# An encoder block's opening: the first norm's gain row loaded into four partitions and spread by VectorE, TensorE given full warming products

## The chip, the core and the metric

The kernel runs on one core of a Trainium2 chip. The core has five engines with instruction queues of their own: TensorE (PE, matrix products; PEld is its weight load), VectorE (DVE), ScalarE (ACT), GpSimd (POOL) and SyncE (SP), which here only issues transfers. SBUF is the memory on chip that the engines work in (128 partitions), PSUM the memory of eight banks that TensorE writes its products to. Sixteen DMA engines move data between the chip's main memory and SBUF; SP, ACT and POOL can issue transfers. Engines wait for one another by semaphores, and each works through its own queue in order.

The metric is device time of one execution in microseconds, the median of several. A profile is one execution, seen by the hardware profiler.

## The reference

A sequence of 512 rows of width 1024 in float32 goes through a feed-forward layer, a mixer (a gated convolution beside a two-way chunked mLSTM) and a second feed-forward layer, each between two RMS norms:

```
def rmsnorm(x, g):
    x32 = x.astype(jnp.float32)
    y = x32 * lax.rsqrt(jnp.mean(x32 * x32, axis=-1, keepdims=True) + EPS)
    return (y * g.astype(jnp.float32)).astype(x.dtype)
...
        h = swiglu(rmsnorm(x, norm_ffn1_pre[l]), w_ffn1_in[l], w_ffn1_out[l])
        x = x + FFN_RESIDUAL_SCALE * rmsnorm(h, norm_ffn1_post[l])
        h = mixer(rmsnorm(x, norm_mix_pre[l]), w_mix_in[l], conv_w[l], ...)
        x = x + rmsnorm(h, norm_mix_post[l])
        h = swiglu(rmsnorm(x, norm_ffn2_pre[l]), w_ffn2_in[l], w_ffn2_out[l])
        x = x + FFN_RESIDUAL_SCALE * rmsnorm(h, norm_ffn2_post[l])
```

The opening, which the change touches, is the very first `rmsnorm(x, norm_ffn1_pre)` and the first columns of `w_ffn1_in`.

## The kernel before

The 512 rows of x stand in four blocks of 128 rows, block 0 to block 3, each a tile of 128 partitions by 1024. A product in float32 is made of three products of the split halves: `split` (L351 on) rounds a tensor to a high part on ScalarE (L352, `whi` for a weight, `big` for activations) and subtracts it for a low part (L355, on VectorE; for the first four weights on GpSimd, `wlo`). TensorE multiplies high by high, high by low and low by high.

The opening runs like this. `pre_norm` normalizes a block: ScalarE squares and sums its two halves (L382), VectorE makes the mean of it (L368, L371), GpSimd takes it to the power -0.5 (L375), and VectorE multiplies x by this scale and by the gain row, half by half (L450). The gain row `norm_ffn1_pre` is one row of 1024 numbers that every partition needs. SyncE loads it into one partition of the tile `g_row` (L321), first in its queue, ahead of x. TensorE spreads it: a product of a column of ones (`vrows`, one partition) with the row, one for each half, puts it into every partition of two PSUM banks, `g_pre` (L348). L450 reads the gain from there for all four blocks.

Around these two products stand 20 warming products of zeros (L345, operand `warm`, a bfloat16 view of `rawg`): 12 ahead of them and 8 behind. Then `flip_q` transposes block 0 and block 1 on TensorE (L407, four transposes to a half), and between the two blocks stand four further transposes into an unused bank (L755). The halves in PSUM are split into the activations' high and low parts (`big`), and a plain copy of them is kept (L413, for blocks 2 and 3 L416). Blocks 2 and 3 are normalized and flipped during the first four weights' products (L524), which take first the columns of blocks 0 and 1 for all four weights, then those of blocks 2 and 3. After that follow the products of a seven-product scheme (L498).

What sets the order: instructions marked `pin` keep the program's order on their engine, others are placed by a scheduler that works with the compiler's own times. SyncE issues g_row, x of blocks 0 and 1 (two halves each), two weights, x of block 2, a weight, x of block 3 and a weight; later weights wait for a free buffer of the pool `raw`. GpSimd's queue has, behind the constants, the powers of blocks 0 and 1, the splits of the first two weights, the power of block 2, the third split, the power of block 3 and the fourth split. The pool `gbp` has two buffers for gains; `g_row` is the first of them, in both kernels.

Of the kernel before, what the change touches and what calls it, by code (L numbers as in the profile page):

```python
# [16 lines left out]
P = 128  # L17
# [9 lines left out]
EPS = 1e-6  # L27
NEG = -1e30
SPLIT = ((8, 5), (8, 5))
WARM = 20  # L30
WARM2 = 4
ON_POOL = (0, 1, 2, 3)
PLAIN = 2
BW = 528
# [4 lines left out]
def encoder_kernel(ctx: ExitStack, tc: tile.TileContext, a: dict, out: bass.AP):  # L39
    nc = tc.nc  # L40
# [15 lines left out]
    def nm(s):  # L56
        uid[0] += 1
        return f"{s}_{uid[0]}"
# [4 lines left out]
    def ps():  # L63
        return psum.tile([P, 512], F32, tag="ps", name=nm("ps"))
# [13 lines left out]
    def blk(i, n=P):  # L78
        return slice(i * n, (i + 1) * n)
# [7 lines left out]
    def pin(ins):  # L87

        if pinned["PE" if ins.ins.engine == nc.tensor.engine else "rest"]:
            tc.keep_in_program_order(ins)  # L90
# [181 lines left out]
    def w_split(n):  # L272
        for _ in range(n):
            if not loaded:
                w_load(1)
            if not loaded:
                return
            raws, kk = loaded.pop(0)
            if isinstance(kk, str):
                ready.append((w_out_a if kk == "a" else w_out_b)(*raws))  # L280
                continue
            if len(raws) == 2:
                ready.append(w_pair(*raws))
                continue
            raw = raws[0]
            hi = wpool.tile([P, 1024], F32R, tag="w", name=nm("whi"))
            lo = wpool.tile([P, 1024], F32R, tag="w", name=nm("wlo"))
            eng = nc.gpsimd if done[0] in ON_POOL else nc.vector
            done[0] += 1
            split(hi, lo, raw, eng)  # L290
            if kk > 1:
                hi, lo = (v.rearrange("p (k f) -> p k f", k=kk) for v in (hi, lo))
            ready.append((hi, lo))
# [12 lines left out]
    def x_load(tb, parts=1):  # L306
        for i in range(parts):
            h = blk(i, D // parts)
            nc.sync.dma_start(x_t[tb][:, h], a["x"][0, blk(tb), h])
# [8 lines left out]
        return g  # L318

    g_row = gbp.tile([P, D], F32, tag="gb", name="g_row")  # L320
    nc.sync.dma_start(g_row[0:1, :], a["norm_ffn1_pre"])  # L321
    x_load(0, 2)
    x_load(1, 2)
    w_load(2)
# [6 lines left out]
    ident = const.tile([P, P], F32, name="ident")  # L331
# [4 lines left out]
    warm = rawg.rearrange("p k f -> p (k f)").bitcast(BF16)  # L336
    nc.gpsimd.memset(warm, 0.0)
    vrows = const.tile([20, P], F32, name="vrows")
    ones = vrows[0:1, :]
    nc.gpsimd.memset(ones, 1.0)  # L340
    pw = ps()
    first = [ps() for _ in range(4)]
    g_pre = [ps() for _ in range(2)]
    for n in range(WARM):
        pin(nc.tensor.matmul(pw[:, 0:256], warm[:, 0:P], warm, start=True, stop=True))  # L345
        if n == 11:
            for i in range(2):
                pin(nc.tensor.matmul(g_pre[i], ones, g_row[0:1, blk(i, 512)], start=True, stop=True))  # L348


    def split(hi, lo, src, eng=nc.vector):  # L351
# [49 lines left out]
    def flip_q(tb, xs, xq, halves=(0, 1), bank=None):  # L401

        full = []
        for b in halves:
            pt = bank or ps()
            for k in range(4):
                pin(nc.tensor.transpose(out=pt[:, blk(k)], in_=xs[:, blk(4 * b + k)], identity=ident))  # L407
            hi, lo = xq_hl(xq, (b, tb // 2))
            split(hi[:, :, blk(tb % 2)], lo[:, :, blk(tb % 2)], ch(pt))
            if b not in xq["f"]:  # L410
                xq["f"][b] = bigt()
            if bank:
                return lambda: pin(nc.vector.tensor_copy(xq["f"][b][:, :, blk(tb)], ch(pt)))  # L413
            full.append((b, pt))
        for b, pt in full:
            pin(nc.scalar.copy(xq["f"][b][:, :, blk(tb)], ch(pt)))  # L416
# [27 lines left out]
    def pre_norm(tb, g, parts=2):  # L444
        xs = t4()
        r = rstd([sumsq(x_t[tb][:, blk(i, D // parts)]) for i in range(parts)], D, 1.0)
        for i in range(2):
            h = blk(i, 512)
            gh = g[i] if isinstance(g, list) else g[:, h]
            pin(nc.vector.scalar_tensor_tensor(  # L450
                out=xs[:, h], in0=x_t[tb][:, h], scalar=r, in1=gh, op0=ALU.mult, op1=ALU.mult))
        return xs
# [295 lines left out]
    xs = [pre_norm(tb, g_pre) for tb in range(2)]  # L748
    full = []
    for tb in range(2):  # L750
        for b in range(2):
            full.append(flip_q(tb, xs[tb], xT1, (b,), first[2 * tb + b]))
        if tb == 0:
            for i in range(WARM2):
                pin(nc.tensor.transpose(out=pw[:, 0:P], in_=xs[0][:, blk(i % 4)], identity=ident))  # L755
        w_split(1)
    for fn in full:
        fn()
# [7 lines left out]
    def rows8(rows, base):  # L766
        v = ident[0:rows, base:base + 64].rearrange("p (d x) -> p d x", d=2)
        return v[:, :, 0:4]
# [3 lines left out]
        out=selc.rearrange("p (d h) -> p d h", d=2), in0=rows8(P, 0), in1=rows8(P, 64), op=ALU.add,  # L772
# [5 lines left out]
        out=pm, in_=selc[0:36].rearrange("p (d h) -> p h d", d=2), axis=AX.X, op=ALU.add,  # L778
# [3 lines left out]
        out=par, in_=selc[0:36].rearrange("p (d h) -> p d h", d=2), axis=AX.X, op=ALU.add,  # L782
# [67 lines left out]
    for tb in range(NT):  # L850
        pv_ = [ps(), ps()]
        n = 0
        for k in range(KD):
# [3 lines left out]
            for xx, ww in ((0, hi), (0, lo), (1, hi)):  # L857
                for i, at in enumerate((slice(0, 256), slice(256, BW))):
                    nc.tensor.matmul(  # L859
                        pv_[i][:, 0:at.stop - at.start], xv(xx, k, tb), ww[:, k % 2, at],  # L860
                        start=n == 0, stop=n == 3 * KD - 1)
# [281 lines left out]
    for c in range(NT):  # L1143
        for pr in range(2):
            nc.tensor.transpose(
                out=pkn[c // 2][:, blk(2 * (c % 2) + pr)], in_=kk_[:, pr, blk(c)], identity=ident,
# [5 lines left out]
    for c in range(NT):  # L1152
# [3 lines left out]
        start=True, stop=True,  # L1156
# [169 lines left out]
    xs = {}  # L1326
    for tb in range(NT):
        acc = [ps(), ps()]
        for half in range(2):
            for n, k in enumerate(MIXK):  # L1330
# [3 lines left out]
                for yi, wi in ((0, 0), (0, 1), (1, 0)):  # L1334
                    nc.tensor.matmul(  # L1335
                        acc[half], yy[yi][:, k % 4, blk(tb)], wmo[k][wi][:, blk(half, 512)],
                        start=(n == 0 and yi == 0 and wi == 0), stop=(n == 7 and yi == 1),
# [40 lines left out]
```

## Time and profile before

| what | value |
|---|---|
| median of 3 runs | 894.24 us (893.87 to 894.26) |
| the profiled execution | 893.36 us |
| its span, first to last instruction | 891.6 us |
| TensorE busy | 883.4 us, 99% |
| VectorE busy | 716.3 us, 80% |
| ScalarE busy | 485.5 us, 54% |
| GpSimd busy | 86.6 us, 10% |
| mean granted TensorE clock | 0.999 |

A row of a timeline has the start from the span's beginning, the length, the engine, the line, the operation, what is written and read, the shapes and the count, and in brackets the engine's idle time ahead of it with what ended it. Rows of the same kind that follow each other are merged, with "x2" and the like. The name `ps` is a PSUM bank, `gb` and `g_row` are gains in SBUF, `t` is a normalized block, `rs` and `ss` are the 128x1 scales and sums.

### The profile page before, as it was taken

To read this page: it belongs to the slowest core of one execution; us is meant where nothing else is said; L and a number is where in the kernel's file an instruction comes from. 1 tells how busy PE (TensorE), PEld (TensorE's weight loads), DVE (VectorE), ACT (ScalarE), POOL (GpSimd) and SP (SyncE) were. 2 spreads that over 40 slices of the span, in tenths; PEclk is the share of its full clock that TensorE was granted. 3 is DMA by queue.
4 is the path that set the end of the run, shared out by engine and by line. 5 is a ranking of instruction groups with operands and counts; after the bars stand their busy time and mean duration, and the time that the engine had idled before them with its cause. 6 is when DMAs were issued, how large, how long until landed. Compare 5 with 4: busy or idle time off the path is not lost.

```text
span 891.6 us, 15212 instructions
## 1 busy us (share of the span) xinstructions
PE 883.4 (99%) x6007; PEld 810.1 (91%) x6007; DVE 716.3 (80%) x1109; ACT 485.5 (54%) x824; POOL 86.6 (10%) x108
## 2 busy tenths in 40 slices
PE   9999999999999999999999999999999999999997
PEld 7999999999988889988888888999999999988885
DVE  5989888888888977688667756898888898797955
ACT  6656455445547645567655535654554555556721
POOL 5000000001140303100111000000000000222000
PEclk9999999999999999999999999999999999999999
DMA  8544434334896651433322621333334324898512
GB/s 238 138 122 118 119 95 115 99 96 122 197 237 181 197 180 73 118 96 105 85 95 89 210 80 56 112 104 109 96 107 127 99 72 142 190 209 220 170 42 93
DMA packets 137234, 114.84 MB, mean 129 GB/s; under 512 B 5173, under 2 KB 115785, under 8 KB 137162
## 3 DMA queue, kind: packets, MB, share of 16 engines
q1 hardware_dynamic: 129354, 97.09, 36.2%
q0 software_dynamic: 7808, 16.78, 9.2%
q8 instruction: 47, 0.77, 0.3%
q14 instruction: 25, 0.20, 0.1%
HBM read 109.66 MB, written 4.19 MB: 128 GB/s over the span
## 4 chain that ended last, share of the span: by engine, by line
PE 98%; DVE 1%; ACT 1%; issue 0%; DVEq 0%; POOLq 0%; POOL 0%; ACTq 0%
PE ps L498 47%; PE ps L651 17%; PE ps L489 10%; PE ps L673 7%; PE ps L1335 5%; PE ps L524 4%; PE ps L859 3%; PE ps L1237 1%; PE ps L407 1%; PE ps L345 1%; PE ps L1245 1%; DVE qt L1107 0%; PE ps L348 0%; PE ps L458 0%; ACT big L352 0%; DVE big L355 0%
## 5 line engine op out<-in xcount | busy, mean ns | idle before, releaser
L498 PE MATMUL ps<-big,whi 128*128 128x256 f32 x2016 | 277.7, 280 | 0.0
L498 PEld LDWEIGHTS ps<-big,whi 128*128 128x128 f32 x2016 | 255.1, 188 | 0.8 <-issue 0.2
L355 DVE TENSOR_TENSOR wlo<-raw,whi 128x1024 fp32r<-128x1024 f32 x165 | 199.9, 1218 | 20.0 <-ACT whi L352 14.0
L352 ACT CAST whi<-raw 128x1024 fp32r<-128x1024 f32 x169 | 174.2, 1050 | 76.0 <-DVE raw L214 30.9
L498 PE MATMUL ps<-big,wlo 128*128 128x256 f32 x1008 | 158.8, 280 | 0.0
L498 PEld LDWEIGHTS ps<-big,wlo 128*128 128x128 f32 x1008 | 136.0, 188 | 0.0
L651 PE MATMUL ps<-whi,big 128*128 128x512 f32 x384 | 119.9, 389 | 0.0
L651 PEld LDWEIGHTS ps<-whi,big 128*128 128x128 f32 x384 | 71.9, 188 | 14.8
L651 PE MATMUL ps<-wlo,big 128*128 128x512 f32 x192 | 74.2, 390 | 0.0
L498 PE MATMUL ps<-big,ws 128*128 128x256 f32 x504 | 68.4, 280 | 0.0
L498 PEld LDWEIGHTS ps<-big,ws 128*128 128x128 f32 x504 | 63.2, 188 | 0.0
L489 PE MATMUL ps<-big,whi 128*128 128x512 f32 x256 | 62.6, 397 | 0.0
L168 POOL DMA_DIRECT2D raw<-in_w_ffn_out_dram x16 | 19.6, 1232 | 435.9 <-DMA raw<-in_w_ffn_out_dram 407.9
L673 PE MATMUL ps<-whi,big 128*128 128x512 f32 x192 | 60.7, 393 | 0.0
L489 PEld LDWEIGHTS ps<-big,whi 128*128 128x128 f32 x256 | 47.6, 188 | 11.1
L576 ACT COPY t<-ps 128x256 f32<-128x256 f32 x40 | 14.9, 372 | 67.1 <-PE ps L498 67.1
L355 DVE TENSOR_TENSOR wlo<-t,whi 128x1024 fp32r<-128x1024 f32 (+1 forms) x42 | 44.7, 1067 | 5.2 <-ACT whi L352 4.8
L352 ACT CAST whi<-t 128x1024 fp32r<-128x1024 f32 (+1 forms) x42 | 38.0, 926 | 18.3 <-DVE t L214 9.7
L673 PEld LDWEIGHTS ps<-whi,big 128*128 128x128 f32 x192 | 36.0, 188 | 8.0
L651 PEld LDWEIGHTS ps<-wlo,big 128*128 128x128 f32 x192 | 36.0, 188 | 7.8 <-DVE wlo L355 0.3
L359 ACT CAST big<-big 128x512 fp32r<-128x512 f32 (+1 forms) x32 | 26.3, 835 | 20.9 <-DVE big L605 10.1
L673 PE MATMUL ps<-wlo,big 128*128 128x512 f32 x96 | 37.6, 392 | 0.0
(233 smaller groups left out, 1323.7 us busy)
## 6 DMA issues: line engine op xcount, KB each, us to landing
raw<-in_w_ffn_in_dram SPq DMA_DIRECT2D x68, 512.0 KB, 4.8
raw<-in_w_ffn_out_dram SPq DMA_DIRECT2D x28, 512.0 KB, 5.2
raw<-in_w_mix_in_dram SPq DMA_DIRECT2D x24, 512.0 KB, 4.0
t<-in_w_ffn_in_dram SPq DMA_DIRECT2D x20, 512.0 KB, 4.6
raw<-in_w_ffn_out_dram SPq DMA_DIRECT2D x32, 256.0 KB, 2.9
raw<-in_w_ffn_out_dram POOLq DMA_DIRECT2D x16, 512.0 KB, 6.9
raw<-in_w_mix_out_dram SPq DMA_DIRECT2D x8, 512.0 KB, 3.5
big<-in_w_ffn_out_dram SPq DMA_DIRECT2D x12, 256.0 KB, 5.5
```

The lines of the kernel that those rows point to most:

```text
L168: nc.gpsimd.dma_start(sums.rearrange("p (g f) -> p g f", g=2), top[:, 512:1024].rearrange("p (g f) -> p g f", g=1).broadcast_to([P, 2, 512 ...
L352: latest["hi"] = nc.scalar.copy(out=hi, in_=src)
L355: latest["lo"] = eng.tensor_tensor(out=lo, in0=src, in1=f32(hi), op=ALU.subtract)
L359: nc.scalar.copy(out=hi, in_=src)
L489: nc.tensor.matmul(o, w[ww][:, k, :], xq_tile(xq, (k // 4, xx))[:, k % 4, FULL], start=n == 0, stop=n == 3 * KD - 1)
L498: pin(nc.tensor.matmul(o, ww[:, k, :], x[xx][:, k, :], start=first and n == 0, stop=n == 11, skip_group_check=True))
L524: pin(nc.tensor.matmul(o, ww[:, k, :], xq_hl(xq, (k // 4, th))[xx][:, k % 4, :], start=n == 0, stop=n == 3 * KD - 1))
L576: nc.scalar.copy(a_[:, h1], x[:, h0])
L651: nc.tensor.matmul(acc[tb + t][half], left[n][x][:, blk(t)], right[n][y], start=first and x == y == 0, stop=last_ and x == 1, skip_group_c ...
L673: nc.tensor.matmul(acc[tb][half], hT[hh][:, blk(tb)], w[ww][:, blk(half, 512)], start=fresh and hh == ww == 0, stop=k == NF - 1 and hh == ...
L859: nc.tensor.matmul(pv_[i][:, 0:at.stop - at.start], xv(xx, k, tb), ww[:, k % 2, at], start=n == 0, stop=n == 3 * KD - 1)
L1335: nc.tensor.matmul(acc[half], yy[yi][:, k % 4, blk(tb)], wmo[k][wi][:, blk(half, 512)], start=(n == 0 and yi == 0 and wi == 0), stop=(n == ...
```

## The change

The gain row is loaded by ScalarE's queue instead of SyncE's, each half into four partitions (0, 32, 64 and 96) of `g_row`, whose halves VectorE has set to zero before. VectorE then spreads each half with a shuffle inside every group of 32 partitions. The two TensorE products, the ones and the two PSUM banks go; all L450 read the gain from `g_row` in SBUF. TensorE's opening has 28 warming products in a row instead of 12 and 8, and six more between the flips of block 0 and block 1 in place of the four unused transposes.

```
-WARM = 20
-WARM2 = 4
+WARM = 28
+WARM2 = 6
...
     g_row = gbp.tile([P, D], F32, tag="gb", name="g_row")
-    nc.sync.dma_start(g_row[0:1, :], a["norm_ffn1_pre"])
+    for i in range(2):
+        nc.vector.memset(g_row[:, blk(i, 512)], 0.0)
+        nc.scalar.dma_start(g_row[0:P:32, blk(i, 512)], a["norm_ffn1_pre"][:, blk(i, 512)].broadcast_to([4, 512]))
     x_load(0, 2)
...
-    ones = vrows[0:1, :]
-    nc.gpsimd.memset(ones, 1.0)
     pw = ps()
     first = [ps() for _ in range(4)]
-    g_pre = [ps() for _ in range(2)]
-    for n in range(WARM):
-        pin(nc.tensor.matmul(pw[:, 0:256], warm[:, 0:P], warm, start=True, stop=True))
-        if n == 11:
-            for i in range(2):
-                pin(nc.tensor.matmul(g_pre[i], ones, g_row[0:1, blk(i, 512)], start=True, stop=True))
+    for i in range(2):
+        pin(nc.vector.stream_shuffle(out=g_row[:, blk(i, 512)], in_=g_row[:, blk(i, 512)], mask=[0] * 32))
+    g_pre = g_row
+
+    def warming(n):
+        for _ in range(n):
+            pin(nc.tensor.matmul(pw[:, 0:256], warm[:, 0:P], warm, start=True, stop=True))
+
+    warming(WARM)
...
         if tb == 0:
-            for i in range(WARM2):
-                pin(nc.tensor.transpose(out=pw[:, 0:P], in_=xs[0][:, blk(i % 4)], identity=ident))
+            warming(WARM2)
```

VectorE's queue from its first instruction to the normalizing of block 0, before (`selc` to `par` are constants of the mixer):

```order
L894 MEMSET gm 36x1
L771 TENSOR_TENSOR selc<-ident 128x8
L775 CAST selp<-selc 128x512
L777 TENSOR_REDUCE pm<-selc 36x4
L781 TENSOR_REDUCE par<-selc 36x2
L368 TENSOR_SCALAR rs_157<-ss_153 128x1
L371 SCALAR_TENSOR_TENSOR rs_159<-ss_155,rs_157 128x1
L450 SCALAR_TENSOR_TENSOR t_20_152<-x_87,rs_161,ps_127 128x512
L450 SCALAR_TENSOR_TENSOR t_20_152<-x_87,rs_161,ps_128 128x512
```

The same place in the changed kernel, where lines stand some three further down:

```order
L322 MEMSET g_row 128x512 x2
L896 MEMSET gm 36x1
L773 TENSOR_TENSOR selc<-ident 128x8
L777 CAST selp<-selc 128x512
L779 TENSOR_REDUCE pm<-selc 36x4
L783 TENSOR_REDUCE par<-selc 36x2
L344 STREAM_SHUFFLE g_row<-g_row 128x512 x2
L371 TENSOR_SCALAR rs_165<-ss_161 128x1
L374 SCALAR_TENSOR_TENSOR rs_167<-ss_163,rs_165 128x1
L453 SCALAR_TENSOR_TENSOR t_18_160<-x_87,rs_169,g_row 128x512 x2
```

The two memsets are new at the front, and the two shuffles stand ahead of block 0's mean; the multiplication reads `g_row` where it read the two banks. Behind this place VectorE's order is that of before.

VectorE's queue at blocks 2 and 3, before:

```order
L368 TENSOR_SCALAR rs_252<-ss_248 128x1
L371 SCALAR_TENSOR_TENSOR rs_254<-ss_250,rs_252 128x1
L450 SCALAR_TENSOR_TENSOR t_47_247<-x_89,rs_256,ps_127 128x512
L450 SCALAR_TENSOR_TENSOR t_47_247<-x_89,rs_256,ps_128 128x512
L368 TENSOR_SCALAR rs_294<-ss_290 128x1
L371 SCALAR_TENSOR_TENSOR rs_296<-ss_292,rs_294 128x1
```

and in the changed kernel:

```order
L371 TENSOR_SCALAR rs_262<-ss_258 128x1
L374 SCALAR_TENSOR_TENSOR rs_264<-ss_260,rs_262 128x1
L453 SCALAR_TENSOR_TENSOR t_45_257<-x_89,rs_266,g_row 128x512 x2
L371 TENSOR_SCALAR rs_304<-ss_300 128x1
L374 SCALAR_TENSOR_TENSOR rs_306<-ss_302,rs_304 128x1
L453 SCALAR_TENSOR_TENSOR t_54_299<-x_90,rs_308,g_row 128x512 x2
```

Nothing has moved here; the operand `ps` has become `g_row`. GpSimd's queue at the same time, in the changed kernel (`wlo` are the low parts of the first four weights):

```order
L378 TENSOR_TENSOR rs_182<-rs_180,nhalf 128x1
L358 TENSOR_TENSOR wlo_209<-raw_104,whi_208 128x1024
L358 TENSOR_TENSOR wlo_225<-raw_106,whi_224 128x1024
L378 TENSOR_TENSOR rs_266<-rs_264,nhalf 128x1
L358 TENSOR_TENSOR wlo_287<-raw_109,whi_286 128x1024
L378 TENSOR_TENSOR rs_308<-rs_306,nhalf 128x1
L358 TENSOR_TENSOR wlo_329<-raw_112,whi_328 128x1024
```

It is the order of before: each power of blocks 2 and 3 is followed by a weight's split. ScalarE's queue begins with the two loads of `g_row` ahead of its table load; SyncE's has lost its first row. PSUM has two banks more to hand round.

## The prediction

> **What bounds the kernel now.** The page first, for the engine that sets the end.
>
> ```profile
> span 891.6 us, 15212 instructions
> PE 98%; DVE 1%; ACT 1%; issue 0%; DVEq 0%; POOLq 0%; POOL 0%; ACTq 0%
> ```
>
> TensorE carries 98% of the chain that ended last, so a change of the opening is worth what it moves TensorE's dense stretch. Where that stretch begins is told by the chain in order of time, cut to the opening (start, length, what).
>
> ```profile
> 1.34 2.74 PE ps L345 x12
> 4.09 3.71 PE ps L348 x4
> 7.79 1.82 PE ps L345 x8
> 9.62 1.72 PE ps L407 x8
> ...
> 27.72 0.61 DVE big L355
> 28.34 0.04 issue
> 28.38 10.13 PE ps L524 x84
> ```
>
> From 28.38 us on TensorE works in one dense stretch, and there it had waited for VectorE's L355, the split of the last flipped block. So 28.38 is the number to move: whatever VectorE's queue loses or wins up to that split, the whole run loses or wins. The timeline of VectorE (DVE) up to it:
>
> ```profile
> 5.24 0.16 DVE L371 SCALAR_TENSOR_TENSOR rs<-ss,rs 128x1 f32<-128x1 f32 x1 [0.60 <-ACT junk L382]
> 6.19 0.75 DVE L450 SCALAR_TENSOR_TENSOR t<-x,rs,ps 128x512 f32<-128x512 f32 x1 [0.79 <-POOL rs L375]
> 7.83 0.75 DVE L450 SCALAR_TENSOR_TENSOR t<-x,rs,ps 128x512 f32<-128x512 f32 x1 [0.90 <-PE ps L348]
> 8.50 0.14 DVE L368 TENSOR_SCALAR rs<-ss 128x1 f32<-128x1 f32 x1
> ...
> 9.65 1.41 DVE L450 SCALAR_TENSOR_TENSOR t<-x,rs,ps 128x512 f32<-128x512 f32 x2 [0.74 <-POOL rs L375]
> ...
> 13.43 1.29 DVE L355 TENSOR_TENSOR big<-ps,big 128x512 fp32r<-128x512 f32 x2 [0.76 <-ACT big L352]
> 14.63 2.47 DVE L413 COPY big<-ps 128x512 f32<-128x512 f32 x4
> 17.02 0.14 DVE L368 TENSOR_SCALAR rs<-ss 128x1 f32<-128x1 f32 x1
> 17.27 0.48 DVE L371 SCALAR_TENSOR_TENSOR rs<-ss,rs 128x1 f32<-128x1 f32 x1
> 18.48 1.41 DVE L450 SCALAR_TENSOR_TENSOR t<-x,rs,ps 128x512 f32<-128x512 f32 x2 [0.73 <-POOL rs L375]
> ...
> 20.06 0.78 DVE L371 SCALAR_TENSOR_TENSOR rs<-ss,rs 128x1 f32<-128x1 f32 x1
> 21.58 1.41 DVE L450 SCALAR_TENSOR_TENSOR t<-x,rs,ps 128x512 f32<-128x512 f32 x2 [0.74 <-POOL rs L375]
> 22.91 1.28 DVE L355 TENSOR_TENSOR big<-ps,big 128x512 fp32r<-128x512 f32 x2
> ```
>
> The four pairs of L450 write the normalized blocks 0 to 3. The second half of block 0 starts at 7.83 after 0.90 us of waiting for L348, TensorE's spread of the gain row. After block 3 (end 21.58 + 1.41 = 22.99) VectorE has no gap up to 28.3. GpSimd's (POOL) timeline in the same stretch:
>
> ```profile
> 9.06 0.56 POOL L375 TENSOR_TENSOR rs<-rs,nhalf 128x1 f32<-128x1 f32 x1 [2.95 <-DVE rs L371]
> 12.97 4.77 POOL L355 TENSOR_TENSOR wlo<-raw,whi 128x1024 fp32r<-128x1024 f32 x2 [3.35 <-ACT whi L352]
> 17.90 0.55 POOL L375 TENSOR_TENSOR rs<-rs,nhalf 128x1 f32<-128x1 f32 x1 [0.16 <-DVE rs L371]
> 18.42 2.41 POOL L355 TENSOR_TENSOR wlo<-raw,whi 128x1024 fp32r<-128x1024 f32 x1
> 20.99 0.56 POOL L375 TENSOR_TENSOR rs<-rs,nhalf 128x1 f32<-128x1 f32 x1 [0.16 <-DVE rs L371]
> 21.51 2.41 POOL L355 TENSOR_TENSOR wlo<-raw,whi 128x1024 fp32r<-128x1024 f32 x1
> ```
>
> Behind each power (L375) of blocks 2 and 3 GpSimd starts a weight split (wlo) of 2.41 us at once, at 18.42 and 21.51, 0.06 us before VectorE's L450 begins. Now the two odd durations of VectorE: L371 on 128x1 takes 0.16 us, but 0.48 at 17.27 (until 17.75; GpSimd's split ended at 12.97 + 4.77 = 17.74) and 0.78 at 20.06 (until 20.84; the split ended at 18.42 + 2.41 = 20.83). L371 reads two tensors in SBUF and was held until GpSimd was done. L450, with the gain in PSUM, ran at its usual 0.7 us a half beside the same splits. The other way round it holds for long instructions too, later in the run:
>
> ```profile
> 301.67 5.43 POOL L810 CAST big<-rawg 128x32 fp32r<-128x32 f32 x1 [25.56 <-PE ps L651]
> ...
> 307.40 0.20 POOL L810 CAST big<-rawg 128x32 fp32r<-128x32 f32 x1
> ```
>
> ```profile
> 305.82 1.22 DVE L355 TENSOR_TENSOR wlo<-raw,whi 128x1024 fp32r<-128x1024 f32 x1
> ```
>
> A copy of 0.20 us on GpSimd lasted 5.43 us, to 307.10, while VectorE ran splits of two SBUF tensors back to back, the last of them, above, to 305.82 + 1.22 = 307.04. So in this trace a VectorE instruction with two SBUF tensors and a GpSimd instruction exclude each other.
>
> **The change, part by part.** *Block 0.* The row is no longer spread by L348, so the second half of block 0 need not wait. Whether the first half stays at 6.19 depends on three small things.
>
> ```profile
> 0.80 1.28 ACT L382 ACT_TABLE_LOAD   x1 [0.80 <-PEq L1365]
> 0.80 0.35 SPq L321 DMA_DIRECT2D g_row<-in_norm_ffn_pre_dram  x1
> ...
> 1.21 1.77 SPq L309 DMA_DIRECT2D x<-in_x_dram  x4
> ...
> 2.00 0.43 DVE L775 CAST selp<-selc 128x512 fp32r<-128x512 f32 x1
> ...
> 3.73 0.63 ACT L382 ACTIVATE junk<-x 128x512 bf16<-128x512 f32 x1 [1.65 <-DMA x<-in_x_dram]
> ```
>
> SyncE drops one issue, so x may start 1.21 - 0.80 = 0.41 us earlier and be there at 3.32 instead of 3.73. ScalarE (ACT) gets two issues ahead of its table load, each behind a memset of VectorE. The memset has no row; its bounds are nothing and the 0.62 us of a copy (2.47 / 4), and I take the 0.43 of the nearest SBUF-to-SBUF row. Two memsets from 0.86 end at about 1.7, two issues of 0.35 at about 2.1, and the table load of 1.28 at 3.4: ScalarE is ready 0.3 us before 3.73; with the upper bound at about 4.1, 0.4 us late. The row's landing plus two shuffles stand in VectorE's queue ahead of L368. An issue at 1.8 to 2.1 with a flight like that of x (1.21 to 3.73, 2.5 us, shared with x's 1 MB) lands by 4.6 at the latest, and two shuffles, taken at a copy's 0.62 us, end at 5.8; a shorter flight ends them before 5.0, where they hide behind ScalarE's squares. So the first half starts between 5.8 and 6.85; I take 6.1. Two halves take 1.41: block 0 ends at **7.5** (7.2 to 8.25) instead of 8.58.
>
> *Warming products.* 28 products at the 2.74 / 12 = 0.228 us of the slow rate would end at 1.34 + 6.4 = 7.7, and earlier once the rate doubles. The flips of block 0 can't begin before 6.9 anyway, so this part sits beside the wait for block 0, as do the six products that replace the four L755 transposes.
>
> *Block 1.* It ended at 11.06, 2.48 us behind block 0, a chain of L368, L371, power and two halves on VectorE and GpSimd alone: 7.5 + 2.48 = 9.98.
>
> *VectorE up to block 2.* Behind block 1 stand four L355 and four L413. Before, the L355 waited for the flips; now TensorE and ScalarE are ahead, and they run dense at the 0.60 us that a pair's start to the next row gives (14.63 - 13.43 = 1.20): 2.40, and the copies 17.02 - 14.63 = 2.39. L368 of block 2 comes at 9.98 - 0.07 + 4.79 = 14.70, and GpSimd's power 0.56 later as in block 1 (8.50 to 9.06), unless a split holds L371: the two splits begin when ScalarE's cast is done, about 9.8, and end before 14.8, just clear. Power of block 2: **15.26** instead of 17.90, 2.64 us earlier.
>
> *Blocks 2 and 3, the new wait.* L450 now reads the gain from SBUF beside x in SBUF: two SBUF tensors, as L371. The instruction itself is not slower.
>
> ```profile
> L450 DVE SCALAR_TENSOR_TENSOR t<-x,rs,gb x16: 741/745/754, 332.5 to 563.0; 128x512 f32<-128x512 f32 x16
> ```
>
> But GpSimd has begun its split 0.52 us after the power's start, and L450 becomes free 0.06 later. I take it that it then waits the whole 2.41 us. From the power's start: 0.52 + 2.41 + 1.35 for two halves = 4.28 to the end of block 2 (before: 1.99). The power of block 3 follows 0.48 later (8.58 to 9.06): 4.76. There GpSimd takes its next split first again: 4.28 more. Block 3 ends 9.04 us after the power of block 2, where it took 22.99 - 17.90 = 5.09. So 3.95 us are lost where 2.64 were won. What is late next: VectorE's dense 28.38 - 22.99 = 5.39 us behind block 3, and TensorE behind that. 15.26 + 9.04 + 5.39 = **29.69**, 1.31 us later than 28.38. TensorE has nothing left to hide it: its own work up to there would be done some two microseconds sooner.
>
> [...]
>
> **Sum.** Against the profiled execution (893.36 us, span 891.6): 893.36 + 1.31 = 894.7. That execution was 0.9 us below the median 894.24 of the runs shown; on the median the sum gives **895.6 us**, 0.15% more. About 0.2%, 1.8 us, is what a measurement of this kernel can tell from no change.
>
> **Rivals.** *Faster: the split doesn't hold L450.* It ran beside GpSimd in this trace, though with PSUM as its second source. Then the 2.64 us stay won, block 3 ends at 15.26 + 5.09 = 20.35, TensorE's stretch starts at 25.74, and some 0.1 to 0.3 us go to TensorE's own work: about -2.5 us, 891.7. Against it stand L371 and the copy of 5.43 us.
>
> *Slower: the full rate comes late.* The rate of TensorE turned late before:
>
> ```profile
> 9.41 1.92 PE L407 MATMUL ps<-ident,t 128*128 128x128 f32 x8
> ...
> 11.97 1.24 PE L407 MATMUL ps<-ident,t 128*128 128x128 f32 x8
> ```
>
> Eight flips took 1.92 us, then 1.24: it turned at about 12.2, 4.4 us after the full products from 7.79 on, while the 2.74 us from 1.34 had not been enough. 28 products in a row give 5.8 by that measure. If they fail all the same, products end at 7.73, flips of block 0 (8 x 0.215) at 9.45, six products at 10.8, flips of block 1 at 12.5; the last L355 then ends about 0.7 us before its old 14.72, and the second split runs to about 16.8 and holds L371. The power of block 2 comes at about 16.9 and TensorE's stretch at 16.9 + 9.04 + 5.39 = 31.3: +3.0, 897.2. It decides if the turn comes after about 9 us. [...]
>
> *Slower: GpSimd's first split comes between the halves of block 1.* The split starts some 2.3 us after block 0's end (transposes, cast, 1.05 us of whi), the second half 1.73 after it. If ScalarE were 0.6 us quicker, that half would wait 2.41 more less what was left: +2.3 on top, 897.9.
>
> **How the numbers follow.** The forecast (the two waits of 2.41 us) has 0.80. Its own range: block 0's end gives -0.3 to +0.75, the halves behind a lock -0.15 to +0.2, so +0.9 to +2.2, or 895.1 to 896.5, with 0.3 on each side between runs. Faster rival 0.12, late rate 0.05, first split 0.03. The low end lies under the forecast's own range, at 894.2; the high end takes in the late rate, 897.2. Outside stay the faster rival, most of the last one and a few hundredths. Faster by over 0.2% (under 892.45): 0.12. Slower by over 0.2% (over 896.03): the late part of the forecast, 0.19 for a block 0 that ends after 7.9, plus 0.08, so 0.27. Within: 0.61.
>
> **What would show it.** Right: in the changed profile L453 of blocks 2 and 3 is one long instruction or idle time of about 3 us that ends 0.7 us after a GpSimd split; block 0 ends near 7.5, block 2's power starts near 15.3, block 3 ends near 24.3, and TensorE's unbroken stretch starts near 29.7. Wrong: all eight L453 take 0.75 us beside the splits (faster rival), or TensorE's flips of block 1 still take 0.2 us each (late rate), or the shuffles end after 6 us, so that block 0 wins nothing.

## The result and the profile after

The changed kernel takes 898.67 us (median of 6 runs, 897.22 to 900.83) where the kernel before took 893.89 beside it (6 runs, 892.91 to 894.26): a ratio of 1.0055, 95% interval 1.0040 to 1.0069. It is 4.8 us slower, where 1.3 to 1.4 had been forecast, and its time lies 1.5 us above the range. A ratio here and below is estimated from the runs and can differ a little from the quotient of the two medians. The profiled execution took 898.28 us.

The head of its page and its chain of waits in order of time, cut to the opening (start, length, what):

```profile
span 896.5 us, 15227 instructions
PE 95%; DVE 3%; issue 0%; DMA 0%; POOL 0%; DVEq 0%; POOLq 0%; ACT 0%; ACTq 0%
```

```profile
2.65 2.93 DMA g_row<-in_norm_ffn_pre_dram
...
5.61 0.72 DVE g_row L344 x2
...
7.38 1.41 DVE t L453 x2
...
11.29 2.39 DVE big L358 x4
13.68 2.39 DVE big L416 x4
...
16.55 0.56 POOL rs L378
...
17.13 3.54 DVE t L453 x2
...
30.68 10.20 PE ps L527 x84
40.88 196.34 PE ps L501 x1668
```

TensorE's share of the chain fell from 98% to 95%: now it is not TensorE that leads through the opening, but the row's transfer and then VectorE. Block 0 ends at 7.38 + 1.41 = 8.79 (before 8.58), so nothing was won there. Block 2's power starts at 16.55 (before 17.90), and the dense stretch at 30.68 (before 28.38), 2.30 us later. Two timelines carry the reason, first VectorE's, then GpSimd's (start, length, engine, line, what, and in brackets the idle time ahead):

```profile
20.85 0.16 DVE L374 SCALAR_TENSOR_TENSOR rs<-ss,rs 128x1 f32<-128x1 f32 x1
21.75 3.54 DVE L453 SCALAR_TENSOR_TENSOR t<-x,rs,g_row 128x512 f32<-128x512 f32 x2 [0.74 <-POOL rs L378]
```

```profile
17.06 2.40 POOL L358 TENSOR_TENSOR wlo<-raw,whi 128x1024 fp32r<-128x1024 f32 x1
...
21.68 2.40 POOL L358 TENSOR_TENSOR wlo<-raw,whi 128x1024 fp32r<-128x1024 f32 x1
```

Where L450 took 1.41 us for two halves beside a split of GpSimd, L453 takes 3.54, at 17.13 and again at 21.75; each time the split has begun 0.07 us ahead. From block 2's power to TensorE's stretch it is now 30.68 - 16.55 = 14.13 us; before it was 28.38 - 17.90 = 10.48. That is 3.65 us lost, against 1.35 won up to the power. And L374 of block 3 has its usual 0.16, since the split ahead of it is over: the hold has passed from the 0.78 us of L371 to the long instruction.

The first profile after has 4.9 us more than the one before, and its opening explains 2.3 of them. The experiments go after both questions: is the exclusion the cause, and where is the rest.

### The profile page after: what moved, and what is told of

Same layout as the page of the kernel before. It is cut to its first block, busy times and chain, and to the rows that moved or that the text cites. A ratio compares the mean times of both kernels' runs of the same rounds, so it can differ in the third digit from the quotient of the medians.

```text
span 896.5 us, 15227 instructions
## 1 busy us (share of the span) xinstructions
PE 883.9 (99%) x6013; PEld 807.8 (90%) x6013; DVE 721.4 (80%) x1115; ACT 485.7 (54%) x824; POOL 86.5 (10%) x107
## 4 chain that ended last, share of the span: by engine, by line
PE 95%; DVE 3%; issue 0%; DMA 0%; POOL 0%; DVEq 0%; POOLq 0%; ACT 0%; ACTq 0%
PE ps L501 46%; PE ps L654 17%; PE ps L492 10%; PE ps L676 7%; PE ps L1337 5%; PE ps L527 4%; PE ps L861 3%; PE ps L1239 1%; DVE t L453 1%; DVE big L358 1%; PE ps L1247 1%; DVE qt L1109 0%; PE ps L410 0%; PE ps L461 0%; DMA g_row<-in_norm_ffn_pre_dram 0%
## 5 line engine op out<-in xcount | busy, mean ns | idle before, releaser
L358 DVE TENSOR_TENSOR wlo<-raw,whi 128x1024 fp32r<-128x1024 f32 x165 | 200.3, 1220 | 19.0 <-ACT whi L355 13.6
L358 DVE TENSOR_TENSOR wlo<-t,whi 128x1024 fp32r<-128x1024 f32 (+1 forms) x42 | 44.8, 1068 | 5.4 <-ACT whi L355 5.0
```

The source lines that it names most:

```text
L358: latest["lo"] = eng.tensor_tensor(out=lo, in0=src, in1=f32(hi), op=ALU.subtract)
```

## The experiments

Times are medians, each beside runs of the kernel before on the same chip. Those took 893.59 us (20 runs) beside the exclusion taken away (called gain23_psum below), the exclusion alone (before_gain23_sbuf), and the two experiments on the queues (row_by_sync and before_row_by_scalar); 893.82 (23 runs) beside the two splits on VectorE, the second profiles and both costs together; 893.88 (9 runs) beside the two on the warming.

**The exclusion taken away from the changed kernel.** ScalarE copies the spread row into two PSUM banks, and blocks 2 and 3 read it there. The theory that is named after a port, here and in the next experiment, is the exclusion; its times are all that the runs show of it.

```
+    g_ps = [ps() for _ in range(2)]
...
-    xs = [pre_norm(tb, g_pre) for tb in range(2)]
+    xs = [pre_norm(0, g_pre)]
+    for i in range(2):
+        pin(nc.scalar.copy(out=g_ps[i], in_=g_row[:, blk(i, 512)]))
+    xs.append(pre_norm(1, g_pre))
...
-        st1[tb] = pre_norm(tb, g_pre)
+        st1[tb] = pre_norm(tb, g_ps)
```

> The changed kernel, with ScalarE copying the spread row into two PSUM banks, from which blocks 2 and 3 read their gain. Theory of the port (a multiplication with two SBUF tensors waits for GpSimd's weight split): both long multiplications of 3.54 us fall back to 1.41, block 3 ends 5.1 us behind block 2's power instead of 8.7, and TensorE's unbroken stretch starts near 27.1 instead of 30.7. The time is 895.1 if the part behind the opening stays as long as in the changed kernel, 892.5 if it is as before. Rival (something else than the split held them, the shuffled gain for one): nothing moves, 898.5.

Measured: 894.28 us (10 runs, 893.22 to 898.9), ratio 1.0017 (1.0002 to 1.0032), 4.4 us under the changed kernel. VectorE's timeline, the split beside it in GpSimd's, and the chain:

```profile
17.48 1.41 DVE L454 SCALAR_TENSOR_TENSOR t<-x,rs,ps 128x512 f32<-128x512 f32 x2 [0.73 <-POOL rs L379]
```

```profile
17.41 2.41 POOL L359 TENSOR_TENSOR wlo<-raw,whi 128x1024 fp32r<-128x1024 f32 x1
```

```profile
24.10 13.41 PE ps L528 x112
37.51 196.23 PE ps L502 x1668
```

The same instruction beside the same split takes 1.41 us again when its second source is in PSUM, in block 3 likewise. The 196-us block of products behind the opening starts at 37.51 instead of 40.88 (before: 38.51). The dense stretch shows earlier than the 27.1 expected because here its row takes in 112 products, not 84; 84 of them (10.13 us in the kernel before) would, by estimate, start at 37.51 - 10.13 = 27.38.

**The exclusion alone, put into the kernel before.** ScalarE copies the two PSUM banks to SBUF, and blocks 2 and 3 read the copy.

```
+    g_sb = gbp.tile([P, D], F32, tag="gb", name="g_sb")
+    for i in range(2):
+        pin(nc.scalar.copy(out=g_sb[:, blk(i, 512)], in_=g_pre[i]))
...
-        st1[tb] = pre_norm(tb, g_pre)
+        st1[tb] = pre_norm(tb, g_sb)
```

> The kernel before, with ScalarE copying the two PSUM banks of the gain into SBUF, from which blocks 2 and 3 read it; nothing else of the change. Theory of the port: two multiplications of about 3.5 us, the stretch starts near 17.9 + 8.7 + 5.4 = 32.0 instead of 28.4, and the time is 897.5, or more if a late opening also lengthens what comes behind. Rival (the long multiplications come from the rest of the change): as before, 894.

Measured: 898.73 us (4 runs, 898.42 to 898.98), ratio 1.0063 (1.0047 to 1.0078). One row each of VectorE, GpSimd and the chain:

```profile
19.18 3.53 DVE L450 SCALAR_TENSOR_TENSOR t<-x,rs,g_sb 128x512 f32<-128x512 f32 x2 [0.73 <-POOL rs L375]
```

```profile
18.59 0.55 POOL L375 TENSOR_TENSOR rs<-rs,nhalf 128x1 f32<-128x1 f32 x1 [0.16 <-DVE rs L371]
19.11 2.39 POOL L355 TENSOR_TENSOR wlo<-raw,whi 128x1024 fp32r<-128x1024 f32 x1
```

```profile
32.71 10.14 PE ps L524 x84
```

With none of the change but the place of the gain, the stretch from power to dense products is 32.71 - 18.59 = 14.12 us, that of the changed kernel to 0.01. That makes 3.64 of the 4.33 us by which the dense products start late; the other 0.69 lie ahead of the power, where one of ScalarE's two copies now stands in the chain. That the median is also that of the changed kernel is a coincidence, since the other parts of the two openings differ.

**The third and fourth split given to VectorE**, so that GpSimd has nothing but the powers beside blocks 2 and 3. The gain stays in SBUF.

```
-ON_POOL = (0, 1, 2, 3)
+ON_POOL = (0, 1)
```

> The changed kernel with ON_POOL = (0, 1): the third and fourth weight's splits (2.41 us each on GpSimd) are made by VectorE. Nothing but the power is then on GpSimd beside blocks 2 and 3. Theory (the exclusion between those splits and L453 costs twice 2.1 us): both L453 pairs take 1.41 us, VectorE pays two splits of 1.22 us instead, so the dense stretch starts 4.3 - 2.4 = 1.9 us earlier, near 28.8, and the first products near 39.0; median near 896.8. Rival (it is the gain's place in SBUF that is slow, whatever GpSimd does): the pairs stay at 3.54 us and the time goes up by the 2.4 us of the two splits, to about 901.

Measured: 895.92 us (10 runs, 894.0 to 898.36), ratio 1.0027 (1.0014 to 1.0041). VectorE's timeline and a row of the chain:

```profile
18.43 1.42 DVE L453 SCALAR_TENSOR_TENSOR t<-x,rs,g_row 128x512 f32<-128x512 f32 x2 [0.73 <-POOL rs L378]
```

```profile
28.79 10.73 PE ps L527 x88
```

With no split of GpSimd beside it, L453 on two SBUF tensors takes 1.42 us, as L450 with its gain in PSUM did (1.41). So in this run the place of the gain costs nothing by itself; the 2.12 us more of the changed kernel (3.54) came with GpSimd's split of 2.40 beside it. The chain's dense stretch starts at 28.79, where 28.8 was expected, but that agreement is partly luck: its row has 88 products here, not 84, and the row landed at 2.64 + 3.92 = 6.56, 1 us later than in the changed kernel's profile. The products behind the opening start at 28.79 + 10.73 = 39.52, against 39.0 expected and 40.88 in the changed kernel.

**The row's loads on SyncE's queue**, the rest as in the changed kernel. The scheduler put them behind block 0's two halves of x and ahead of block 1's.

```
-        nc.scalar.dma_start(g_row[0:P:32, blk(i, 512)], ...)
+        nc.sync.dma_start(g_row[0:P:32, blk(i, 512)], ...)
```

> The changed kernel with the row's two loads issued by SyncE instead of ScalarE. Theory of the late row: ScalarE's table load moves up by 2 us and the second shuffle ends 0.5 to 1 us sooner, so block 0 ends near 8 instead of 8.8 and the stretch starts that much sooner, near 29.8. Theory that ScalarE's transfer queue slows what comes later: the part behind the opening falls from 865.9 to 863.3, and the time is near 895. Rival (the part behind the opening is longer for another reason): 897.7.

Measured: 896.16 us (5 runs, 895.76 to 897.82), ratio 1.0038 (1.0020 to 1.0055). VectorE's timeline, and a row of the chain:

```profile
4.81 0.75 DVE L344 STREAM_SHUFFLE g_row<-g_row 128x512 f32<-128x512 f32 x1
...
6.60 1.41 DVE L453 SCALAR_TENSOR_TENSOR t<-x,rs,g_row 128x512 f32<-128x512 f32 x2 [0.74 <-POOL rs L378]
```

```profile
29.88 10.14 PE ps L527 x84
```

ScalarE's squares start at 3.28 here instead of 4.49, the second shuffle at 4.81 instead of 5.61; block 0 ends at 6.60 + 1.41 = 8.01 instead of 8.79, and the stretch starts 0.80 us earlier. The median gains 2.5 us, more than that; the second profile of the changed kernel below, whose opening is another 1.55 us longer, accounts for part of the difference.

**ScalarE's queue alone.** The kernel before, with its one load issued by ScalarE.

```
-    nc.sync.dma_start(g_row[0:1, :], a["norm_ffn1_pre"])
+    nc.scalar.dma_start(g_row[0:1, :], a["norm_ffn1_pre"])
```

> The kernel before with the one load of the row issued by ScalarE instead of SyncE; nothing else. Theory that the use of ScalarE's transfer queue slows later transfers: the part behind the opening grows from 863.3 by about 2.6 and the time is 896.5. Rival (the queue is harmless): 894, with x up to 0.4 us earlier.

Measured: 893.62 us (10 runs, 891.08 to 895.61), ratio 1.0006 (0.9993 to 1.0018). Using that queue costs this kernel nothing that was measured.

**Second profiles of both kernels**, to separate what is steady from what scatters.

> The kernel before, unchanged, for a second profile. Theory (the full rate turns now early, now late in this opening, 4.8 us in before_row_by_scalar and 12.4 us in the profile shown, and what an early opening wins the output stages mostly give back): the dense stretch starts anywhere between 23 and 28.4 us, the first products between 36.7 and 38.5, and the rest behind them is longer where they start early, so that the total stays at 891.5 to 894.8. Rival (before's opening is always that of its profile): the dense stretch at 28.4, the first products at 38.5 within 0.2, and the rest 850.2 us.

> The changed kernel, unchanged, for a second profile. Theory (the 2.6 us that it lost behind its opening are the scatter of the weights' transfers in the two output stages): the first products start at 40.9 within 0.3, and the rest behind them differs from the first profile's 852.3 us by up to 2. Rival (the 2.6 us are a steady effect of the change): the rest is 852.3 within 0.3, with the same two steps of 1.0 us in the output stages.

Measured: 894.06 and 897.80 us. Of the chain of the kernel before, then of the changed kernel:

```profile
28.16 10.14 PE ps L524 x84
```

```profile
2.65 4.12 DMA g_row<-in_norm_ffn_pre_dram
...
32.23 10.14 PE ps L527 x84
42.37 196.23 PE ps L501 x1668
```

Before, the opening came out the same within 0.22 us. After, it is another 1.55 us longer, 32.23 against 30.68. Most of it is the row, which landed at 2.65 + 4.12 = 6.77 instead of 5.58. The rest is TensorE's clock: in stretches of the opening (length, PE busy, granted clock, where a clock of 1.00 before its first turn only means that no record exists), first of the repeat, then of the first profile:

```profile
6.40:9.80 3.40, 1.06 (x10) 1.00 1.06 302
9.80:13.20 3.40, 3.40 (x18) 0.51 0.95 288
```

```profile
6.00:9.40 3.40, 2.02 (x17) 1.00 1.09 305
```

In the repeat TensorE had 2.34 us without work between the warming products and the flips, and the clock stood at half from 9.8 to 13.2, in most of the flips of both blocks. In the first profile it kept its rate.

Behind the opening the picture turned round. From the start of the dense stretch to the execution's end the first pair has 893.36 - 28.38 = 864.98 and 898.28 - 30.68 = 867.60 us, the second 894.06 - 28.16 = 865.90 and 897.80 - 32.23 = 865.57. The 2.6 us that the first pair lost behind the opening did not come back; with two profiles of each they pass for scatter, but for one steady piece. The chain's last row, before and after:

```profile
888.02 0.66 DVEq L1374
```

```profile
892.50 0.66 DVEq L1376
```

From its end to the execution's end it is 893.36 - 888.68 = 4.68 us before and 898.28 - 893.16 = 5.12 after. In the other three profiles built on the kernel before it is 4.66, in the other seven built on the changed one 5.10 to 5.13. So 0.45 us are lost behind the last store's issue; no run tells by what.

**The warming.** First more of it, so that TensorE isn't idle before the flips; then that of before (20 products, four unused transposes).

```
-WARM = 28
+WARM = 42
```

> The changed kernel with 42 warming products in a row instead of 28, so that TensorE is busy until block 0's flips (8.2 us in the changed kernel's profile, where the 28 ended at 6.8; in the second profile they ended at 7.0, the flips came at 9.4, and the granted clock stood at half from 9.8 to 13.2 us, which made the opening 1.5 us longer). Theory (the late row leaves TensorE idle between the warming products and the flips, and in about half of the executions the clock then falls back): the products end at 8.3 to 9.3, no half clock between the turn and the run's end, the dense stretch at 30.7 within 0.3, the median 0.5 to 1.0 under that of the changed kernel, 897.7 to 898.2, with fewer executions near 900. Rival (the dip is rare or costs nothing in the median, since the output stages' waits are larger): 898.7 as before, or more, as the longer warming delays block 0's flips.

```
-WARM = 28
+WARM = 20
...
-            warming(WARM2)
+            for i in range(4):
+                pin(nc.tensor.transpose(out=pw[:, 0:P], in_=xs[0][:, blk(i % 4)], identity=ident))
```

> The changed kernel with the warming of before: 20 products (not interrupted now, as the spread products are gone) and the four unused transposes between the flips of blocks 0 and 1. It undoes the third part of the change alone. Theory (what counts is whether TensorE is at full rate in the flips; 20 products end at 5.9 at the slow rate and leave 2.3 us idle before the flips at 8.2): the clock turns early only in some executions and falls back in some, the flips take 0.2 us each at half rate, the dense stretch starts 0 to 1.5 us later, between 30.7 and 32.2, and the median is 0.3 to 1.0 higher, 899.0 to 899.7. Rival (block 0 is so late that the flips are not what VectorE waits for): median 898.7 within 0.3.

Measured: 899.30 us (5 runs, 897.15 to 900.45), ratio 1.0060 (1.0047 to 1.0072) with 42 products, and 898.22 (5 runs, 897.26 to 899.58), ratio 1.0055 (1.0041 to 1.0069) with the old warming. Neither differs from the changed kernel by more than the intervals. The chain with 42 products:

```profile
2.65 3.66 DMA g_row<-in_norm_ffn_pre_dram
...
31.42 10.20 PE ps L527 x84
```

With 42 products the clock was full from 5.2 us to the end of the run, and the stretch still started 0.74 us later than in the changed kernel's first profile, because the row landed 0.73 later (2.65 + 3.66 = 6.31). With the old warming the stretch started at 31.39; the clock fell to half from 9.5 to 12.9, and that cost about 0.33: from block 0's end (9.16) to the stretch it is 31.39 - 9.16 = 22.23, against 30.68 - 8.79 = 21.89. So the theory written down for the 42 products, that the half clock makes 1.5 us, fell: it makes 0.3 to 0.4, and the row's landing makes the rest.

**Both costs taken away together**: the row on SyncE's queue, and the gain of blocks 2 and 3 from PSUM (the edits of row_by_sync and gain23_psum).

> The changed kernel with two edits together: the row's two loads are issued by SyncE, as in row_by_sync, and blocks 2 and 3 read the gain from two PSUM banks that ScalarE copies, as in gain23_psum. Theory (two independent costs: the exclusion on L453 of blocks 2 and 3, and a row that lands late): block 0 ends near 8.0 us plus 0.3 for the two copies, the power of block 2 comes near 16.1, each L453 pair of blocks 2 and 3 takes 1.41 us again, block 3 ends near 21.2, the first products behind the opening start near 36.7 (37.51 in gain23_psum, 40.02 in row_by_sync); median 0.8 us under gain23_psum, about 893.4. Rival (an opening that ends before about 38 us gains nothing, since the output stages wait for their weights' transfers anyway): the opening is as early, and the median stays at 894.3 or above.

Measured: 892.52 us (12 runs, 892.14 to 894.10 but for one of 3093.09, which nothing on record explains and which the ratio leaves out), ratio 0.9989 (0.9981 to 0.9998): 6 us under the changed kernel, and 0.1% under the one before, which is less than the 0.2% set as the bound of no change. The chain:

```profile
10.21 0.66 PE ps L411 x4
...
23.29 13.38 PE ps L528 x112
36.68 196.23 PE ps L502 x1668
```

The products behind the opening start at 36.68 against 36.7 expected, and the median is 0.9 us under the 893.4 expected. From 10.21 on TensorE itself is the chain, without a gap: this opening can now be shortened only by what brings those flips forward. In gain23_psum they began 0.8 us later (11.02), and 37.51 - 36.68 = 0.83.

## Why the prediction failed, step by step

**What held.** The exclusion, on which the forecast rested with 0.80, is right in place and nearly in length, shown by taking it away in two ways and by putting it in alone; what makes it no run shows. From block 2's power to the stretch it said 9.04 + 5.39 = 14.43; it is 14.13 (8.74 + 5.39). Block 1 ends 2.50 behind block 0 (said: 2.48), VectorE's dense L358 and L416 and the power come as the sum had them: 16.55 - 8.79 = 7.76 from block 0's end to block 2's power (15.26 - 7.5 = 7.76). That a split holds up a 512-wide instruction for the whole 2.41 us was the author's estimate from L371 (0.48 and 0.78 us where it usually takes 0.16), and no row of the trace before showed it; the runs show 3.54 us for the two halves beside a split of 2.40 and 1.42 without, so 2.12 more.

**What failed: the term of block 0.** It said 7.5, at most 8.25, with a chance of 0.19 for anything after 7.9. In the four profiles of the changed kernel and its two warming variants it is 8.79, 9.98, 9.53 and 9.16. The start of ScalarE's timeline shows the first of two misses:

```profile
1.50 1.67 ACTq L323 DMA_DIRECT2D g_row<-in_norm_ffn_pre_dram  x2
3.20 1.28 ACT L385 ACT_TABLE_LOAD   x1 [3.20 <-DVE par L783]
4.49 0.63 ACT L385 ACTIVATE junk<-x 128x512 bf16<-128x512 f32 x1
...
5.79 0.19 ACT L385 ACTIVATION_READ_ACCUMULATOR junk<-x 128x1 f32 x1
```

An issue was put at 0.35 us, the price of SyncE's row; these two took 1.67 together, so ScalarE was ready at 4.48 instead of 3.4, and block 0's squares, which began then without a wait, ended at 5.98. That alone puts block 0's end near 8.4, an estimate (5.98 and the 2.46 us by which 8.79 lies behind the shuffles' end at 6.33). The queue alone is not the reason: one load of the whole row took 0.51 us on it (before_row_by_scalar), and the same two loads took 1.22 on SyncE's (row_by_sync); what lengthens the issue no run separates. The second miss comes on top, some 0.3 us in the first profile and 1.5 in the repeat: the row was said to land by 4.6 at the latest, and its second half landed at 5.58 to 6.77, 2.4 to 3.6 us behind the end of its issue, while SyncE's transfers were on their way. So two shuffles that were to hide behind ScalarE's squares were what VectorE waited for. Both misses shrink when the loads change queue: in row_by_sync block 0 ends at 8.01. A late row was named only as a sign ("the shuffles end after 6 us"); it should have been a rival with a price, since no row of the trace before showed a transfer issued at that place by that queue.

**What was not foreseen.** The late row also leaves TensorE idle, and the clock that the warming products had raised fell again in some of these openings: to 0.51 behind the 2.34 us without work in the repeat, and to 0.50 with the two splits on VectorE (10.7 to 14.1) and with the old warming (9.5 to 12.9). That cost 0.3 to 0.4 us, an estimate from the repeat (1.55 less the row's 6.77 - 5.58 = 1.19) and the old warming (0.33). (It turned at 6.0 where 5.8 was said, but that was luck: with the warming products in a row it turned anywhere from 4.2 to 7.3 us.) The medians with the old warming and with 42 products differ from that with 28 by less than the intervals, so in this kernel the change's third part is worth nothing that was measured.

**The account.** Against the profile of before, the stretch was to start 1.31 later; it starts 2.30 and (second pair) 4.07 later. Of the 0.99 missing in the first pair block 0's end makes 1.29 (ScalarE's late start some 0.95, the row the rest) and the part behind block 2's power -0.30. The mean of the two openings, 3.2 us, and the 0.45 at the end give 3.6 of the 4.8 us between the medians. Both profiled executions of the changed kernel (898.28, 897.80) lie under its median, so later rows in the executions without a profile may make the remaining 1.1 us; that stays open. The premise that the whole run loses or wins what the opening does is only roughly borne out: the products behind the opening start at 36.68 to 42.85 us in the twelve profiles, and from there to the execution's end it takes 854.9 to 857.4 us in eleven of them, and 859.4 in gain23_psum, where the clock fell in mid-run.

## What to carry to other kernels

Before an operand moves from PSUM to SBUF, look at what GpSimd runs beside its reader: here 1.35 us won ahead of block 2's power did not pay for two pairs of instructions that beside a split of 2.40 us took 3.54 each instead of 1.41. When a load is given to another queue and tied to a memset, price it by where it lands behind the traffic already issued (here 5.58 to 6.77 us where 4.6 had been said), and let its latest landing be a case with a price. A second profile of each kernel tells a loss from scatter more cheaply than an argument does.

## What the runs showed of the hardware

- TensorE's granted clock stood at half for 3.41 us with the two splits on VectorE (10.69 to 14.10) and for 3.41 in gain23_psum (270.41 to 273.82, below), and at full for 887.47 us in the first profile of the changed kernel and 877.23 in that of the kernel before, which is 260 and 257 times 3.413. Such a stretch of 3.41 us is called a step here. The clock fell to half behind a step in which TensorE was busy for 1.06 us (6.4 to 9.8 in the repeat above, 0.51 behind it), for 0.93 (6.1 to 9.5 in the old warming, 0.50 behind it) and for 1.67 (7.3 to 10.7 with the two splits on VectorE, 0.50 behind it), and stayed at 1.00 behind one with 2.02 (6.0 to 9.4 in the first profile of the changed kernel) and one with 1.77 (4.17 to 7.58 in gain23_psum). If one bound separates these five, it lies between 1.67 and 1.77, an estimate from them alone. The longer gap was not the one that cost the clock: that of 1.72 us with the two splits (7.46 to 9.18) fell into one step, and the clock fell behind it; that of 2.60 in gain23_psum (5.94 to 8.54) was shared by two steps, and it did not. The stretches, of the two splits on VectorE and of gain23_psum:

```profile
7.30:10.70 3.40, 1.67 (x13) 1.00 1.05 313
10.70:14.10 3.40, 3.21 (x16) 0.50 1.08 342
```

```profile
4.17:7.58 3.41, 1.77 (x16) 1.00 0.75 230
7.58:10.99 3.41, 1.97 (x14) 1.00 1.06 298
```

- A dip came in mid-run too. In the profile of gain23_psum, TensorE waited 2.44 us for a weight's high part, the clock stood at 0.50 from 270.41 to 273.82, behind a step with 1.32 us busy, and the products, 0.23 us apart ahead of the wait, came 0.43 apart behind it:

```profile
267.70 0.39 PE L655 MATMUL ps<-wlo,big 128*128 128x512 f32 x1
267.93 0.39 PE L655 MATMUL ps<-whi,big 128*128 128x512 f32 x1
270.75 2.07 PE L655 MATMUL ps<-whi,big 128*128 128x512 f32 x4 [2.44 <-ACT whi L356]
272.62 0.63 PE L655 MATMUL ps<-wlo,big 128*128 128x512 f32 x1
273.05 0.63 PE L655 MATMUL ps<-whi,big 128*128 128x512 f32 x1
```

- The clock first turned at different times under the same 28 products, which start at 1.35 us: at 4.17 in gain23_psum and at 7.28 with the two splits on VectorE. Counted back from there by 3.41 us, an estimate since no clock is on record ahead of the first turn, the step from 0.76 held 2.8 us of them in gain23_psum, and the one that ended at 3.87 with the two splits held 2.5 and was followed by no turn. In before_gain23_sbuf it turned at 13.23, behind 3.41 us (9.82 to 13.23) that held nothing but transposes (L407 and L758). In the kernel before it turned at 12.4 and 10.8, and at 4.8 in before_row_by_scalar, where the spread products L348 took 2.34 us instead of 3.78 and the products behind the opening started at 36.77 instead of 38.51. Yet that execution took 892.92 us, only 0.44 less than the first: its chain has a wait of 1.56 us at 265.33, ahead of a weight's rounding on ScalarE, that the first profile's chain lacks.

```profile
4.01 2.34 PE L348 MATMUL ps<-g_row,vrows 1*128 1x512 f32 x4
```
